# Forty-two instead of thirty-two tokens leave the dense expert grid of a PEER layer, and their expert rows are gathered in three zero-filled parts of 768 columns

## The chip, the cores and the metric

The kernel runs on one core of a Trainium2 chip. The metric is device time in microseconds (us) of one execution, the median of several. A core has TensorE (PE in the rows; its weight loads are PEld), VectorE (DVE), ScalarE (ACT), GpSimd (POOL) and SyncE (SP). SP issues the plain transfers here, POOL the gathers by index. All transfers run on the core's 16 DMA engines.

## The reference

One layer of a decoder trunk over 256 tokens of width 2048, all in float32. A token mixer (sliding-window attention and an mLSTM, gated and summed) comes first, and the change leaves it alone. Then comes PEER, a product-key retrieval of single-neuron experts:

```python
x = x + peer(rms_norm(x, norm_ffn_g), w_peer_q, peer_keys, peer_u, peer_v)

def peer(xn, w_peer_q, peer_keys, peer_u, peer_v):
    qp = (xt @ w_peer_q).reshape(T, 8, 2, 128)
    scores = einsum('thcd,hcnd->thcn', qp, peer_keys)      # 2 x 128 keys a head
    s_top, i_top = top_k(scores, 16)
    top_s, pos = top_k(sums of the two halves, 16)          # 16 of 256 pairs
    idx = ...                                               # i0 * 128 + i1, of 16384 experts
    gates = softmax(top_s)
    act = gelu(einsum('td,thkd->thk', xb, peer_u[idx]))
    return einsum('thk,thkd->td', gates * act, peer_v[idx])
```

Each token thus uses 8 x 16 = 128 of the 16384 rows of `peer_u` and of `peer_v`, each row 2048 wide.

## The kernel before

The kernel takes two ways through PEER. For most tokens it doesn't gather: it multiplies *all* 16384 rows of `peer_u` with all these tokens (the dense grid), multiplies the result with a grid of gates that is zero where a token did not choose an expert, and multiplies this grid with all of `peer_v`. The first `SP` = 32 tokens leave the grid (`ND = T - SP` = 224 stay): their 128 rows each are gathered by an indirect DMA.

**The dense grid.** `run` walks a list of units. A unit is one weight tile of 128 x 1024 floats (512 KB): SP loads it into `raw` (4 buffers, L94), ACT rounds it to `hi` (L89), DVE forms `lo = raw - hi` (L90; 2 buffers of each), and PE multiplies 8 pieces of `hi` with the tokens' high and low halves side by side (2 x ND = 448 columns) and 8 pieces of `lo` with the high half (ND = 224 columns). There are 512 units: 256 of `u` (L824, L829), then 256 of `v` (L1101, L1103). `run` emits the load and split of unit n+1 ahead of PE's work of unit n.

**What runs between.** After each unit `step` emits other work, counted by two paces: `rows_todo` (one gathered row of each of the leaving tokens; it takes `ROW` off the other pace) and `side` (choosing the experts, then `scatter`, which builds the grid of gates four tokens at a time with 4 matmuls of 128 x 128, 8 instructions on PE, L1040). In the first 92 units of `u` the choice of experts runs beside; in the other 164 `scatter` and the rows of `u`. Every fourth unit of `v` splits four rows of the grid into `ring` (`split_w`, 4 x ND elements a partition).

**The leaving tokens.** Their rows lie in `PARTS` = 4 parts of `HD` = 512 columns on 4 x 32 = 128 partitions. `fetch` gathers, for choice s, one row part a partition into one of 5 slabs; `dot` (DVE, L957) multiplies it with `own["x"]` and sums along the row; `own_weights` adds the parts with a small matmul and forms the weights; `add_row` (DVE, L983) adds the rows of `v`. There are 128 gathers of `u` and 128 of `v`; in the `v` units one every 1.81 units (`NS / (len(units) - 24)` = 128/232 a unit).

**The ends.** 40 units into the second half of `v`, `load_x1` brings back the residual in three pieces on SP's queue: tokens SP..127 (`n0` = 96 rows of 8 KB), tokens 128..255, and the leaving tokens' parts. Three units before the end `own_out` adds and stores the leaving tokens. `finish` then transposes, adds and stores the dense tokens: for each of 4 column blocks one store of `n0` rows and one of 128 rows, 2 KB a row. A plain transfer of SP waits for the eighth one before it as well (a semaphore of eight in turn).

Of the kernel before, what the change touches and what calls it, by code (L numbers as in the profile page):

```python
# [8 lines left out]
F32 = mybir.dt.float32  # L9
# [4 lines left out]
OP = mybir.AluOpType  # L14
AX = mybir.AxisListType
# [10 lines left out]
PH, NK, TOPK = 8, 128, 16  # L26
NE = NK
# [2 lines left out]
LOW = -3.0e38  # L30
HU = 1024
QU = 512
SP = 32
ND = T - SP
PARTS = P // SP
HD = D // PARTS
ROW = 0.75


@with_exitstack  # L40
def hybrid_block_kernel(ctx: ExitStack, tc: tile.TileContext, a, out):
    nc = tc.nc
    V, S, G, PE = nc.vector, nc.scalar, nc.gpsimd, nc.tensor
# [12 lines left out]
    ident = cst.tile([P, P], F32, name="ident")  # L56
# [72 lines left out]
    def step(parts, consume, rate):  # L129
# [343 lines left out]
    for t in range(NT):  # L473
        ts = slice(t * P, (t + 1) * P)
        for g in range(4):
            src = aqk[:, t, g * 256:(g + 1) * 256].rearrange("p (h d) -> p h d", d=DH)
            V.tensor_mul(src, src, rq[:, t, g * 4:(g + 1) * 4].unsqueeze(2).to_broadcast([P, 4, DH]))
            ps = psd.tile([P, QU], F32, name="sd")
# [8 lines left out]
        ps = psd.tile([P, QU], F32, name="sd")  # L487
# [237 lines left out]
    i0T = exc.tile([P, T], F32, name="i0T")  # L725
    i1T = exc.tile([P, T], F32, name="i1T")
    part = exc.tile([P, 1], F32, name="part")
    for c in range(PARTS):
        V.memset(part[c * SP:(c + 1) * SP], float(c))
    pair = exc.tile([P, SP], F32, name="pair")  # L730
    V.tensor_reduce(pair, ident.rearrange("p (c t) -> p t c", c=PARTS), axis=AX.X, op=OP.add)
    NSL = 5
    slab = [exc.tile([P, HD], F32, name=f"slab{j}") for j in range(NSL)]
    NA = 80
# [51 lines left out]
    W = [wA, None]  # L786
# [4 lines left out]
    done = {"tok": 0, "e": 0}  # L791
# [15 lines left out]
    own = {}  # L807
# [99 lines left out]

    tables = {"u": a["ur"], "v": a["v"].rearrange("e (c d) -> (e c) d", d=HD)}  # L910
# [13 lines left out]

    def fetch(table, s):
        ix = own["ix"]
        G.indirect_dma_start(out=slab[s % NSL], out_offset=None, in_=tables[table],  # L927
                             in_offset=bass.IndirectOffsetOnAxis(ap=ix[:, s:s + 1], axis=0))

    def quarter_rows(dst, src):  # L930

        for c in range(PARTS):
            G.dma_start(dst[c * SP:(c + 1) * SP], src[:, c * HD:(c + 1) * HD])

    def own_x():
        quarter_rows(own["x"], x1d[0:SP])
        g = a["grow"]
        quarter_rows(slab[NSL - 1], bass.AP(tensor=g.tensor, offset=g.offset, ap=[[0, SP], [1, D]]))

    def own_index():  # L940
        V.tensor_mul(own["x"], own["x"], slab[NSL - 1])
        ef = tk.tile([SP, NS], F32, name="ef")
        V.scalar_tensor_tensor(ef, iv[0:SP, 0], float(NK), iv[0:SP, 1], op0=OP.mult, op1=OP.add)
        G.dma_start(exd, ef)
        for c in range(PARTS):
            G.dma_start(own["ixf"][c * SP:(c + 1) * SP], exd)

    def own_rows():
        V.tensor_scalar(own["ixf"], own["ixf"], float(PARTS), part, op0=OP.mult, op1=OP.add)
        V.tensor_copy(own["ix"], own["ixf"])  # L950
        for s in range(NSL):
            fetch("u", s)
        rows_todo.extend([lambda s=s: dot(s) for s in range(NS)])

    def dot(s):
        sl = slab[s % NSL]
        (V.scalar_tensor_tensor(sl, sl, 1.0, own["x"], op0=OP.mult, op1=OP.mult,  # L957
                                    accum_out=own["dots"][:, s:s + 1]))
        if s + NSL < NS:
            fetch("u", s + NSL)  # L960

    def own_weights():
        zt, wt, wgt = own["zt"], slab[0][:, 0:NS], own["dots"]
        zp = psd.tile([P, QU], F32, name="sd")
        PE.matmul(zp[:, 0:SP], own["dots"], pair, start=True, stop=True)
        yield
        V.tensor_mul(zt, zp[:, 0:SP], rb[:, 0:SP])
        S.activation(zt, zt, AF.Gelu)
        V.tensor_mul(wt.rearrange("p (c t) -> p c t", c=PARTS), zt.unsqueeze(1).to_broadcast([P, PARTS, SP]),
                     gT[:, 0:SP].unsqueeze(1).to_broadcast([P, PARTS, SP]))  # L970
        yield
        wp = psd.tile([P, QU], F32, name="sd")
        PE.transpose(wp[:, 0:NS], wt, ident)
        V.tensor_copy(wgt, wp[:, 0:NS])
        for s in range(NSL):
            fetch("v", s)

    def add_row(s):
        w = own["dots"][:, s:s + 1]
        if s == 0:  # L980
            (V.tensor_scalar(own["x"], slab[0], w, None, op0=OP.mult))
        else:
            (V.scalar_tensor_tensor(own["x"], slab[s % NSL], w, own["x"], op0=OP.mult, op1=OP.add))  # L983
# [40 lines left out]
    TG = 4  # L1024

    def scatter(t0):

        A = eb.tile([P, TG, NK], F32, name="A")
        B = eb.tile([P, TG, NK], F32, name="B")
        V.tensor_tensor(A, iot.unsqueeze(1).to_broadcast([P, TG, NK]),  # L1030
                        i0T[:, t0:t0 + TG].unsqueeze(2).to_broadcast([P, TG, NK]), op=OP.is_equal)
        for j in range(TG):
            t = t0 + j
            S.activation(B[:, j], iot, AF.Square, bias=i1T[:, t:t + 1])
            S.activation(B[:, j], B[:, j], AF.Relu, bias=gT[:, t:t + 1], scale=ngT[:, t:t + 1])  # L1035
            if j % 2:
                yield
        ps = psd.tile([P, TG, NK], F32, name="sd")
        for j in range(TG):
            PE.matmul(ps[:, j], B[:, j], A[:, j], start=True, stop=True)  # L1040
        yield
        m = done["e"]
        c0 = t0 - SP
        for mul, s in ((False, 0), (False, 1), (True, 0), (True, 1)):
            lo, hi = ((0, NA), (NA, NE))[s]
            for x0, x1 in (((lo, min(max(m, lo), hi)),) if mul else ((max(min(m, hi), lo), hi),)):
                if x1 <= x0:
                    continue
                dst = W[s][:, x0 - lo:x1 - lo, c0:c0 + TG]
                src = ps[:, :, x0:x1].rearrange("p t i -> p i t")  # L1050
# [169 lines left out]
```

## Time and profile before

| | |
|---|---|
| median of 3 runs | 2179.22 us (2178.59 to 2179.59) |
| the profiled execution, its own time | 2179.96 us |
| its span, first to last instruction | 2178.2 us |
| PE busy, weight loads busy | 97%, 89% of the span |
| DVE, ACT, POOL busy | 77%, 60%, 18% |
| bytes moved | 487.22 MB, 224 GB/s over the span |

The span is what the rows of the trace cover; the profiled execution's own time is 1.8 us longer. Matmuls are pipelined, so PE's busy share is no measure of how far it is from its peak: its pace is read from where one matmul starts and where the next does. An engine that is busy all the time sets the pace only where others wait for it.

### The profile page before, as it was taken

The page shows a single profiled execution, that of the slowest core. Times are in us where ns is not written, and L with a number is a line of the kernel's source. Part 1 is how long each engine was busy: PE and PEld are TensorE (multiplying, and loading weights), DVE is VectorE, ACT ScalarE, POOL GpSimd, SP SyncE. Part 2 cuts the span into 40 slices and gives each one's busy share as a digit, 9 for nine tenths or more (in the row PEclk, how much of TensorE's full clock was granted, in tenths as well). Part 3 has the DMA queues.
Part 4 walks back from the last instruction along what each step waited for, and adds up shares of the span by engine and source line. Part 5 has one row for each costly group of instructions (what it writes and reads, how often), then busy time and mean ns, then how long its engine had stood idle before and what let it go on. Part 6 is the DMA issues. An engine that isn't in the chain of part 4 may idle for free. (4 is left out here: it accounts for less than half of the span.)

```text
span 2178.2 us, 34889 instructions
## 1 busy us (share of the span) xinstructions
PE 2120.5 (97%) x12836; PEld 1934.2 (89%) x12836; DVE 1685.0 (77%) x2915; ACT 1307.7 (60%) x2269; POOL 382.4 (18%) x324
## 2 busy tenths in 40 slices
PE   6999999999999999998999999999999999999997
PEld 5887778888888888997999999998999999989997
DVE  7987688878887889898777777886777777767765
ACT  5755566556644455555889888886455455545453
POOL 3000000000022002102332333321222222222200
PEclk9999999999999999999999999999999999999999
DMA  5565544555577545765777677776887777888764
GB/s 202 187 190 175 163 155 165 175 190 187 185 253 265 178 174 198 243 222 182 251 251 261 239 251 254 259 238 210 270 267 266 268 270 257 270 272 272 265 229 141
DMA packets 138892, 487.22 MB, mean 224 GB/s; under 512 B 17713, under 2 KB 19969, under 8 KB 138241
## 3 DMA queue, kind: packets, MB, share of 16 engines
q1 hardware_dynamic: 115520, 415.43, 56.0%
q0 software_dynamic: 20896, 67.73, 10.0%
q8 instruction: 100, 1.64, 0.3%
q10 hardware_dynamic: 2304, 1.84, 0.3%
q14 instruction: 72, 0.58, 0.1%
HBM read 478.88 MB, written 6.05 MB: 223 GB/s over the span
## 5 line engine op out<-in xcount | busy, mean ns | idle before, releaser
L90 DVE TENSOR_TENSOR lo<-raw,hi 128x1024 fp32r<-128x1024 f32 x762 | 936.6, 1230 | 423.2 <-ACT hi L89 416.3
L89 ACT ACTIVATE hi<-raw 128x1024 fp32r<-128x1024 f32 x762 | 804.6, 1058 | 759.5 <-PE mm L1101 312.8
L824 PE MATMUL mm<-X,hi 128*128 128x448 f32 x2048 | 467.5, 371 | 11.4 <-ACT hi L89 8.9
L824 PEld LDWEIGHTS mm<-X,hi 128*128 128x128 f32 x2048 | 367.7, 190 | 38.8 <-ACT hi L89 12.5
L1101 PE MATMUL sd<-X,hi 128*128 128x448 f32 x1024 | 378.6, 370 | 11.4 <-ACT hi L89 8.8
L1101 PE MATMUL mm<-X,hi 128*128 128x448 f32 x1024 | 376.8, 368 | 0.0
L174 PE MATMUL mm<-X,hi 128*128 128x512 f32 x1040 | 271.1, 402 | 15.1 <-ACT hi L89 8.4
L829 PEld LDWEIGHTS mm<-X,lo 128*128 128x128 f32 x2048 | 268.2, 192 | 14.2 <-DVE lo L90 7.6
L829 PE MATMUL mm<-X,lo 128*128 128x224 f32 x2048 | 270.0, 274 | 4.1 <-DVE lo L90 4.0
L1103 PE MATMUL mm<-X,lo 128*128 128x224 f32 x1024 | 243.2, 276 | 0.0
L1103 PE MATMUL sd<-X,lo 128*128 128x224 f32 x1024 | 241.3, 273 | 0.0
L174 PEld LDWEIGHTS mm<-X,hi 128*128 128x128 f32 x1040 | 189.5, 191 | 53.2 <-DVE X L90 9.0
L927 POOL DMA_INDIRECT slab<-v,oix x128 | 149.4, 1167 | 474.2 <-DVE ox L983 415.1
L927 POOL DMA_INDIRECT slab<-ur,oix x128 | 150.8, 1178 | 402.9 <-DVE slab L957 367.5
L1101 PEld LDWEIGHTS sd<-X,hi 128*128 128x128 f32 x1024 | 194.6, 190 | 23.3 <-ACT hi L89 9.2
L1101 PEld LDWEIGHTS mm<-X,hi 128*128 128x128 f32 x1024 | 194.7, 190 | 13.3
L1103 PEld LDWEIGHTS sd<-X,lo 128*128 128x128 f32 x1024 | 197.0, 192 | 3.9
L1103 PEld LDWEIGHTS mm<-X,lo 128*128 128x128 f32 x1024 | 197.0, 192 | 2.8
L178 PEld LDWEIGHTS mm<-X,lo 128*128 128x128 f32 x1040 | 142.7, 191 | 10.4
L178 PE MATMUL mm<-X,lo 128*128 128x256 f32 x1040 | 146.4, 283 | 0.0
L1035 ACT ACTIVATE B<-B,gT,ngT 128x128 f32<-128x128 f32 x224 | 110.8, 494 | 7.5
L700 POOL COPY sqa<-sq 128x256 f32<-128x256 f32 x1 | 0.9, 875 | 564.3 <-ACT sq L698 564.3
(326 smaller groups left out, 2441.4 us busy)
## 6 DMA issues: line engine op xcount, KB each, us to landing
raw<-u SPq DMA_DIRECT2D x256, 512.0 KB, 4.4
raw<-v SPq DMA_DIRECT2D x256, 512.0 KB, 4.6
raw<-w_g SPq DMA_DIRECT2D x64, 512.0 KB, 3.5
raw<-w_tok SPq DMA_DIRECT2D x56, 512.0 KB, 3.6
raw<-w_qk SPq DMA_DIRECT2D x32, 512.0 KB, 3.6
raw<-w_o SPq DMA_DIRECT2D x32, 512.0 KB, 3.8
raw<-w_pq SPq DMA_DIRECT2D x32, 512.0 KB, 3.7
raw<-w_pa SPq DMA_DIRECT2D x16, 512.0 KB, 3.2
```

The lines of the kernel that those rows point to most:

```text
L89: S.activation(hi, src, AF.Copy)
L90: V.tensor_sub(lo, src, hi.bitcast(F32))
L174: PE.matmul(ps, hi[:, w], X[:, k].rearrange("p s t -> p (s t)"), start=(k == 0), stop=False)
L178: PE.matmul(ps[:, :T], lo[:, w], X[:, k, 0], start=False, stop=(k == kts - 1))
L700: G.tensor_copy(sqa, sq)
L824: PE.matmul(ps[:, :2 * ND], hi[:, w], Xn[:, k].rearrange("p s t -> p (s t)"), start=(k == 0), stop=False)
L829: PE.matmul(ps[:, :ND], lo[:, w], Xn[:, k, 0], start=False, stop=(k == KT - 1))
L927: G.indirect_dma_start(out=slab[s % NSL], out_offset=None, in_=tables[table], in_offset=bass.IndirectOffsetOnAxis(ap=ix[:, s:s + 1], axis=0))
L1035: S.activation(B[:, j], B[:, j], AF.Relu, bias=gT[:, t:t + 1], scale=ngT[:, t:t + 1])
L1101: PE.matmul(acc[h][j][:, :2 * ND], hi[:, j * P:(j + 1) * P], both, start=(i == 0), stop=False)
L1103: PE.matmul(acc[h][j][:, :ND], lo[:, j * P:(j + 1) * P], ring[:, i % NR, 0], start=False, stop=(i == NE - 1))
```

## The change

`SP` goes from 32 to 42, so `ND` from 224 to 214. `PARTS` goes from 4 to 3 and `HD` from 512 to 768; 3 x 42 = 126 partitions (`PU`) are used. 3 x 768 = 2304 is more than 2048, so the host lays out both tables with rows filled up with zeros (`ur`, `vr`); the third part of a row holds 512 columns of data and 256 zeros, and the gather moves them all. `ROW`, the row's share in the pace, goes from 0.75 to 1.03. `part` (which part a partition holds) now comes from an iota and two comparisons, and `own["x"]` and one slab are set to zero before they are filled. `scatter` takes 214 tokens in 53 groups of four and one of two. `n0` goes from 96 to 86.

```diff
-SP = 32
+SP = 42
 ND = T - SP
-PARTS = P // SP
-HD = D // PARTS
-ROW = 0.75
+PARTS = 3
+PU = PARTS * SP
+HD = 768
+ROW = 1.03
...
-    tables = {"u": a["ur"], "v": a["v"].rearrange("e (c d) -> (e c) d", d=HD)}
+    tables = {"u": a["ur"], "v": a["vr"]}
+    ends = [(c * HD, min(c * HD + HD, D)) for c in range(PARTS)]
...
-        G.indirect_dma_start(out=slab[s % NSL], out_offset=None, in_=tables[table],
-                             in_offset=bass.IndirectOffsetOnAxis(ap=ix[:, s:s + 1], axis=0))
+        G.indirect_dma_start(out=slab[s % NSL][0:PU], out_offset=None, in_=tables[table],
+                             in_offset=bass.IndirectOffsetOnAxis(ap=ix[0:PU, s:s + 1], axis=0))
...
     def own_x():
+        V.memset(own["x"], 0.0)
+        V.memset(slab[NSL - 1], 0.0)
...
-        sl = slab[s % NSL]
-        (V.scalar_tensor_tensor(sl, sl, 1.0, own["x"], op0=OP.mult, op1=OP.mult,
-                                    accum_out=own["dots"][:, s:s + 1]))
+        sl = slab[s % NSL][0:PU]
+        V.scalar_tensor_tensor(sl, sl, 1.0, own["x"][0:PU], op0=OP.mult, op1=OP.mult,
+                               accum_out=own["dots"][0:PU, s:s + 1])
...
-            (V.scalar_tensor_tensor(own["x"], slab[s % NSL], w, own["x"], op0=OP.mult, op1=OP.add))
+            V.scalar_tensor_tensor(ox, sl, w, ox, op0=OP.mult, op1=OP.add)
...
         for c in range(PARTS):
-            nc.sync.dma_start(x1s[c * SP:(c + 1) * SP], x1d[0:SP, c * HD:(c + 1) * HD])
+            c0, c1 = ends[c]
+            nc.sync.dma_start(x1s[c * SP:(c + 1) * SP, 0:c1 - c0], x1d[0:SP, c0:c1])
...
-        "ur": z["peer_u"].reshape(PARTS * NE * P, HD),
+        "ur": fill(z["peer_u"]),
+        "vr": fill(z["peer_v"]),
```

The line numbers move with the change: L824 becomes L828, L957 L965, L983 L991, L1080 L1091, L1101 L1113, L1103 L1115, L1120 L1132.

On SP the transfers around `load_x1` stood so before (`raw` is the weight buffer, `wA` the tile whose front part the residual reuses, `x1d` the residual in DRAM):

```order
L94 DMA raw<-v 128x1024 x170
L1080 DMA wA<-x1d 96x2048
L1081 DMA wA<-x1d 128x2048
L1083 DMA wA<-x1d 32x512 x4
L94 DMA raw<-v 128x1024 x85
L1125 DMA out<-ox 32x512 x4
L94 DMA raw<-v 128x1024
L1120 DMA out<-wA 96x512
L1120 DMA out<-wA 128x512
```

and so they stand now:

```order
L95 DMA raw<-v 128x1024 x170
L1091 DMA wA<-x1d 86x2048
L1092 DMA wA<-x1d 128x2048
L1095 DMA wA<-x1d 42x768 x2
L1095 DMA wA<-x1d 42x512
L95 DMA raw<-v 128x1024 x85
L1138 DMA out<-ox 42x768 x2
L1138 DMA out<-ox 42x512
L95 DMA raw<-v 128x1024
L1132 DMA out<-wA 86x512
L1132 DMA out<-wA 128x512
```

Nothing moved in place: the same 170 and 85 loads of `v` stand around the residual. The row counts did: 96 became 86, and four pieces of 32 rows became three of 42.

On DVE a piece of the `v` units stood so before (`lo` is the split of a weight tile, `X` the split of four grid rows, `ox` the sum of the leaving tokens):

```order
L983 SCALAR_TENSOR_TENSOR ox<-slab_6803,odots,ox 128x512
L90 TENSOR_TENSOR lo<-raw,hi 128x1024
L90 TENSOR_TENSOR X<-wB,X 128x4x224
L90 TENSOR_TENSOR lo<-raw,hi 128x1024
L983 SCALAR_TENSOR_TENSOR ox<-slab_6799,odots,ox 128x512
```

and now:

```order
L991 SCALAR_TENSOR_TENSOR ox<-slab_6804,odots,ox 126x768
L91 TENSOR_TENSOR lo<-raw,hi 128x1024
L91 TENSOR_TENSOR X<-wB,X 128x4x214
L91 TENSOR_TENSOR lo<-raw,hi 128x1024
L991 SCALAR_TENSOR_TENSOR ox<-slab_6800,odots,ox 126x768
```

The order is the same; the row operation has 768 instead of 512 elements a partition, the grid split 856 instead of 896.

## Rows read from the trace of the kernel before

**Rows 1.** Page: busy; a queue's packets, MB, share; chain; issues, us to landing.

```profile
PE 2120.5 (97%) x12836; PEld 1934.2 (89%) x12836; DVE 1685.0 (77%) x2915; ACT 1307.7 (60%) x2269; POOL 382.4 (18%) x324
...
q1 hardware_dynamic: 115520, 415.43, 56.0%
...
PE sd L1101 10%; PE mm L1101 9%; PE mm L1103 5%; PE sd L1103 5%; DMA raw<-v 1%; DVE wA L1119 0%; ACT hi L89 0%; DVE wA L215 0%; SPq L1125 0%; DVE lo L90 0%; DVE ox L1123 0%; DVEq L1216 0%; DVE ox L983 0%; DVE oT L215 0%; ACT wA L214 0%
...
raw<-v SPq DMA_DIRECT2D x256, 512.0 KB, 4.6
```

**Rows 2.** Windows, three stages: busy us (instructions), clock, DMA share, GB/s.

```profile
790.00:1015.00 225.00, 220.63 (x1391) 207.31 (x1390) 206.92 (x485) 121.61 (x180) 43.19 (x24) 1.00 0.63 214
1050.00:1450.00 400.00, 394.37 (x2597) 375.26 (x2596) 316.09 (x618) 341.84 (x799) 129.34 (x110) 1.00 0.76 255
1550.00:1900.00 350.00, 349.91 (x2224) 332.84 (x2223) 256.41 (x258) 178.62 (x183) 90.13 (x77) 1.00 0.79 267
```

**Rows 3.** Timeline of PE, one unit of v: start, duration, instruction.

```profile
1700.54 0.38 PE L1101 MATMUL sd<-X,hi 128*128 128x448 f32 x1
...
1702.17 0.27 PE L1103 MATMUL sd<-X,lo 128*128 128x224 f32 x1
...
1703.05 0.38 PE L1101 MATMUL sd<-X,hi 128*128 128x448 f32 x1
```

**Rows 4.** Timeline of PE, a unit of the output projection.

```profile
621.50 2.03 PE L174 MATMUL mm<-mx__4427,hi 128*128 128x512 f32 x8
623.37 1.09 PE L178 MATMUL mm<-mx__4427,lo 128*128 128x256 f32 x8
624.30 0.38 PE L681 MATMUL sd<-ident,xt 128*128 128x128 f32 x2
```

**Rows 5.** Timeline of PE, a unit of u and a scatter.

```profile
1301.75 1.05 PE L829 MATMUL mm<-X,lo 128*128 128x224 f32 x8
1302.63 1.06 PE L1040 MATMUL sd<-A,B 128*128 128x128 f32 x8
1303.45 1.87 PE L824 MATMUL mm<-X,hi 128*128 128x448 f32 x8
```

**Rows 6.** Groups by form, 1050 to 1450: busy us, mean ns, idle before.

```profile
L824 PE MATMUL mm<-X,hi 128*128 128x448 f32 x1104 | 252.0, 370 | 5.2 <-ACT hi L89 4.7
...
L90 DVE TENSOR_TENSOR lo<-raw,hi 128x1024 fp32r<-128x1024 f32 x139 | 170.3, 1225 | 78.8 <-ACT hi L89 78.3
...
L957 DVE SCALAR_TENSOR_TENSOR slab<-slab,ox 128x512 f32<-128x512 f32 x110 | 75.1, 683 | 0.0
```

**Rows 7.** Groups by form, 1490 to 2150.

```profile
L983 DVE SCALAR_TENSOR_TENSOR ox<-slab,odots,ox 128x512 f32<-128x512 f32 x127 | 94.8, 746 | 0.0
```

**Rows 8.** Waits of PE, 780 to 1040: total us, times, longest.

```profile
PE mm L829 <- DVE lo L90: 4.0, 7, 1.5
```

**Rows 9.** Timeline of SP around the residual's load.

```profile
1924.76 0.47 SPq L1080 DMA_DIRECT2D wA<-x1d  x1
1925.27 0.49 SPq L1081 DMA_DIRECT2D wA<-x1d  x1
```

**Rows 10.** The chain that ended last, at this place.

```profile
1928.46 12.82 DMA raw<-v
1941.38 1.07 ACT hi L89
```

**Rows 11.** Windows behind it.

```profile
1938.00:1940.00 2.00, 0.00 (x0) 0.00 (x0) 0.00 (x0) 0.00 (x0) 0.00 (x0) 1.00 1.00 321
1940.00:1942.00 2.00, 0.00 (x0) 0.00 (x0) 0.00 (x0) 0.62 (x1) 0.00 (x0) 1.00 1.03 412
...
1944.00:1946.00 2.00, 2.00 (x8) 1.83 (x7) 2.00 (x3) 0.56 (x2) 0.37 (x1) 0.50 0.70 254
```

**Rows 12.** DMA, 1924 to 1942: packets; issues with KB and us to landing.

```profile
DMA packets 1436, 5.59 MB, mean 310 GB/s; under 512 B 232, under 2 KB 232, under 8 KB 1212
```

**Rows 13.** DMA, 2168 to 2179, the last stores.

```profile
DMA packets 1024, 1.84 MB, mean 167 GB/s; under 512 B 128, under 2 KB 128, under 8 KB 1024
...
out<-wA SPq DMA_DIRECT2D x4, 256.0 KB, 3.4
out<-wA SPq DMA_DIRECT2D x4, 192.0 KB, 3.1
```

**Rows 14.** Timeline of SP at the end.

```profile
2169.28 4.76 SPq L1120 DMA_DIRECT2D out<-wA  x8
```

More of the change, by code (lines that the diff above doesn't have):

```diff
@@ L727, in hybrid_block_kernel @@
     part = exc.tile([P, 1], F32, name="part")
-    for c in range(PARTS):
-        V.memset(part[c * SP:(c + 1) * SP], float(c))
+    pcol = exc.tile([P, 1], F32, name="pcol")
+    G.iota(pcol, pattern=[[0, 1]], base=0, channel_multiplier=1, allow_small_or_imprecise_dtypes=True)
+    V.tensor_scalar(part, pcol, float(SP), None, op0=OP.is_ge)
+    V.tensor_scalar(pcol, pcol, float(2 * SP), None, op0=OP.is_ge)
+    V.tensor_add(part, part, pcol)
     pair = exc.tile([P, SP], F32, name="pair")
-    V.tensor_reduce(pair, ident.rearrange("p (c t) -> p t c", c=PARTS), axis=AX.X, op=OP.add)
+    V.tensor_reduce(pair, ident[:, 0:PU].rearrange("p (c t) -> p t c", c=PARTS), axis=AX.X, op=OP.add)
     NSL = 5
@@ L926, in fetch @@
         ix = own["ix"]
-        G.indirect_dma_start(out=slab[s % NSL], out_offset=None, in_=tables[table],
-                             in_offset=bass.IndirectOffsetOnAxis(ap=ix[:, s:s + 1], axis=0))
+        G.indirect_dma_start(out=slab[s % NSL][0:PU], out_offset=None, in_=tables[table],
+                             in_offset=bass.IndirectOffsetOnAxis(ap=ix[0:PU, s:s + 1], axis=0))
     def quarter_rows(dst, src):
         for c in range(PARTS):
-            G.dma_start(dst[c * SP:(c + 1) * SP], src[:, c * HD:(c + 1) * HD])
+            G.dma_start(dst[c * SP:(c + 1) * SP, 0:ends[c][1] - ends[c][0]], src[:, ends[c][0]:ends[c][1]])
     def own_x():
+        V.memset(own["x"], 0.0)
+        V.memset(slab[NSL - 1], 0.0)
         quarter_rows(own["x"], x1d[0:SP])
@@ L940, in own_index @@
     def own_index():
-        V.tensor_mul(own["x"], own["x"], slab[NSL - 1])
+        V.tensor_mul(own["x"][0:PU], own["x"][0:PU], slab[NSL - 1][0:PU])
         ef = tk.tile([SP, NS], F32, name="ef")
@@ L948, in own_rows @@
     def own_rows():
-        V.tensor_scalar(own["ixf"], own["ixf"], float(PARTS), part, op0=OP.mult, op1=OP.add)
-        V.tensor_copy(own["ix"], own["ixf"])
+        V.tensor_scalar(own["ixf"][0:PU], own["ixf"][0:PU], float(PARTS), part[0:PU], op0=OP.mult, op1=OP.add)
+        V.tensor_copy(own["ix"][0:PU], own["ixf"][0:PU])
         for s in range(NSL):
@@ L964, in own_weights @@
         zp = psd.tile([P, QU], F32, name="sd")
-        PE.matmul(zp[:, 0:SP], own["dots"], pair, start=True, stop=True)
+        PE.matmul(zp[:, 0:SP], own["dots"][0:PU], pair[0:PU], start=True, stop=True)
         yield
@@ L968, in own_weights @@
         S.activation(zt, zt, AF.Gelu)
-        V.tensor_mul(wt.rearrange("p (c t) -> p c t", c=PARTS), zt.unsqueeze(1).to_broadcast([P, PARTS, SP]),
+        V.tensor_mul(wt[:, 0:PU].rearrange("p (c t) -> p c t", c=PARTS), zt.unsqueeze(1).to_broadcast([P, PARTS, SP]),
                      gT[:, 0:SP].unsqueeze(1).to_broadcast([P, PARTS, SP]))
@@ L972, in own_weights @@
         wp = psd.tile([P, QU], F32, name="sd")
-        PE.transpose(wp[:, 0:NS], wt, ident)
-        V.tensor_copy(wgt, wp[:, 0:NS])
+        PE.transpose(wp[0:PU, 0:NS], wt[:, 0:PU], ident)
+        V.tensor_copy(wgt[0:PU], wp[0:PU, 0:NS])
         for s in range(NSL):
@@ L978, in add_row @@
     def add_row(s):
-        w = own["dots"][:, s:s + 1]
+        w, sl, ox = own["dots"][0:PU, s:s + 1], slab[s % NSL][0:PU], own["x"][0:PU]
         if s == 0:
-            (V.tensor_scalar(own["x"], slab[0], w, None, op0=OP.mult))
+            V.tensor_scalar(ox, sl, w, None, op0=OP.mult)
         else:
-            (V.scalar_tensor_tensor(own["x"], slab[s % NSL], w, own["x"], op0=OP.mult, op1=OP.add))
+            V.scalar_tensor_tensor(ox, sl, w, ox, op0=OP.mult, op1=OP.add)
         if s + NSL < NS:
@@ L1026, in scatter @@
     def scatter(t0):
+        tg = min(TG, T - t0)
         A = eb.tile([P, TG, NK], F32, name="A")
         B = eb.tile([P, TG, NK], F32, name="B")
-        V.tensor_tensor(A, iot.unsqueeze(1).to_broadcast([P, TG, NK]),
-                        i0T[:, t0:t0 + TG].unsqueeze(2).to_broadcast([P, TG, NK]), op=OP.is_equal)
-        for j in range(TG):
+        V.tensor_tensor(A[:, 0:tg], iot.unsqueeze(1).to_broadcast([P, tg, NK]),
+                        i0T[:, t0:t0 + tg].unsqueeze(2).to_broadcast([P, tg, NK]), op=OP.is_equal)
+        for j in range(TG + 1):
+            if j in (2, TG):
+                yield
+            if j >= tg:
+                continue
             t = t0 + j
@@ L1035, in scatter @@
             S.activation(B[:, j], B[:, j], AF.Relu, bias=gT[:, t:t + 1], scale=ngT[:, t:t + 1])
-            if j % 2:
-                yield
         ps = psd.tile([P, TG, NK], F32, name="sd")
-        for j in range(TG):
+        for j in range(tg):
             PE.matmul(ps[:, j], B[:, j], A[:, j], start=True, stop=True)
@@ L1048, in scatter @@
                     continue
-                dst = W[s][:, x0 - lo:x1 - lo, c0:c0 + TG]
-                src = ps[:, :, x0:x1].rearrange("p t i -> p i t")
+                dst = W[s][:, x0 - lo:x1 - lo, c0:c0 + tg]
+                src = ps[:, 0:tg, x0:x1].rearrange("p t i -> p i t")
                 if mul:
@@ L1054, in scatter @@
                     S.activation(dst, src, AF.Copy)
-        done["tok"] = c0 + TG
+        done["tok"] = c0 + tg
     side += [(0.55, scatter(t0)) for t0 in range(SP, T, TG)]
@@ L1122, in own_out @@
     def own_out():
-        V.tensor_add(own["x"], own["x"], x1s)
+        V.tensor_add(own["x"][0:PU], own["x"][0:PU], x1s[0:PU])
         for c in range(PARTS):
-            nc.sync.dma_start(out[0:SP, c * HD:(c + 1) * HD], own["x"][c * SP:(c + 1) * SP])
+            c0, c1 = ends[c]
+            nc.sync.dma_start(out[0:SP, c0:c1], own["x"][c * SP:(c + 1) * SP, 0:c1 - c0])
     units = [(a["v"][i * P:(i + 1) * P, h * HU:(h + 1) * HU], v_consume(i, h)) for h in range(2) for i in range(NE)]
@@ L1177, in col, with fill @@
         return v.reshape(-1, P).T
+    def fill(m):
+        return np.pad(m, ((0, 0), (0, PARTS * HD - D))).reshape(-1, HD)
     wt = np.concatenate([cols(w, 0, 3), cols(w, 5, 7)], axis=1)
```

## The prediction

> **What bounds the kernel now.** I read the page first. The chain that ended last is almost wholly PE in the lines of the `v` units [rows 1], so what counts is how fast PE gets from one unit to the next, and which waits break that. The table by stage comes next [rows 2]. A unit has 16 matmuls, so 1550 to 1900 holds 2224/16 = 139 units, 2.52 us each, with no idle PE. From 1050 to 1450 there are 1104/8 = 138 units of `u` [rows 6], 2.90 us each, scatter's matmuls included, and 5.6 us of idle PE. From 790 to 1015, where the experts are chosen, DVE is busy 206.9 of 225 us, a unit takes 2.59 us, and in and around this stretch PE waited seven times for DVE's `lo` [rows 8]: there DVE is nearly as tight as PE. The transfer engines are busy 0.79 of the time at 267 GB/s in `v` [rows 2].
>
> Then PE's timeline, start to start, since a matmul's own duration is no pace. In `v`, eight matmuls of 448 columns take 1702.17 - 1700.54 = 1.63 us (204 ns each) and eight of 224 take 0.88 us (110 ns) [rows 3]. Before the grid, eight of 512 take 1.87 us (234 ns) and eight of 256 take 0.93 us (116 ns) [rows 4]. Eight of 128 columns in scatter still take 0.82 us (102 ns), beside eight of 224 in 0.88 [rows 5]. So long matmuls follow their columns, short ones hardly.
>
> **What PE saves.** Two parts to each unit:
>
> - `hi`, 448 to 428 columns. Between 448 and 512 a column costs (234 - 204)/64 = 0.47 ns, so 20 columns 9.4 ns; in proportion it is 204 x 20/448 = 9.1. I take 9.2.
> - `lo`, 224 to 214. In proportion it would be 4.9 ns; between 224 and 256 ten columns cost 2.0 ns, between 128 and 224 only (110 - 102)/96 x 10 = 0.8 ns. 214 lies in the last interval: 0.8.
>
> [...]
>
> By stage: 256 units of `v` save 20.5 us, the 164 later units of `u` 13.1. The first 92 would save 7.4; there DVE is 92% busy and gets longer rows, so I keep half, 3.7. Scatter has 53.5 groups instead of 56, 2.5 x 0.82 us = 2.0 [rows 5]. Together -39.3.
>
> **What DVE pays.** The row operation takes 683 ns for 512 elements, the split 1225 for 1024 [rows 6]: 1.06 ns an element, so 256 more cost 0.27 us; `add_row`, 746 ns now [rows 7], becomes about 1.02 us. In `v` DVE has 256.4/139 = 1.84 us a unit, plus 0.552 x 0.27 = 0.15: 1.99 of 2.43, so it hides behind PE with 0.4 us to spare. In the later `u` it has 316.1/138 = 2.29, plus 110/138 x 0.27 = 0.21: 2.50 of some 2.80, 90%. That still fits on average, but scatter's work comes in lumps and DVE works in order: an `lo` stands behind a longer row operation. I charge 4 us (0 to 10). The two memsets, the iota and comparisons: 1 us, in the stretch where DVE is tight.
>
> **What the gathers pay.** A gather grows from 262 KB to 126 x 3 KB = 387 KB; 256 of them are 32 MB more. In `v` a unit then needs 524 + 0.552 x 387 = 738 KB in 2.43 us, 304 GB/s. At 0.79 busy for 267 GB/s the engines would be full at 338, so 304 is 0.90 of them. The only stretch in which everything waits for transfers ran at 310 GB/s [rows 12], which leaves 2%. Five slabs give a gather five turns of 1.81 units, 22 us, so a later landing there stalls nobody; what is at risk is the weight tile, which lands in 4.6 us [rows 1]. It has four buffers and is issued three units ahead, 7 us: slack enough on average. I charge 2 us (0 to 10).
>
> **The row counts 86.** This is the unknown. Each large plain transfer of the `v` stage before has a row count that is a multiple of 16: 128, 96, 32 rows. The last stores show what one costs in packets: 4 x 96 + 4 x 128 = 896 rows and 1024 packets, so 128 small ones, 16 to each of eight stores [rows 13]: every one of them ended on 16 engines. 86 = 2 x 43 can't be shared evenly among 16; among engines that get the same number of whole rows it goes over two. No row shows whether the split must be even. Lower bound: as now, nothing. Upper bound: two engines.
>
> - *The residual's load.* Now its 96 rows put 6 x 8 KB on each engine. Over two engines it is 43 x 8 KB = 352 KB on each. An engine moves 412/16 = 25.7 GB/s at the best [rows 11] and 415.43 MB/(0.56 x 16 x 2178.2 us) = 21.3 on average [rows 1]: 13.7 to 16.5 us instead of about 2. The next weight tiles are queued behind it on SP's queue [rows 9]. [...] I take 10.
> - *The stores.* From SP's first issue at 2169.28 [rows 14] the span lasts 8.9 us. Over two engines the four stores of 86 rows put 4 x 43 x 2 KB = 352 KB on each, 13.7 to 16.5 us, and the four of 128 rows 64 KB more, 2.5 to 3 us. With 3.5 us for start and landing (a store lands in 3.1 us with almost nothing to move [rows 13]) that is 20 to 23 us instead of 8.9: 11 to 14. I take 12; nothing on PE can cover it, it is the end.
>
> I take the even split, since all that the rows show is even. [...]
>
> The pieces of 42 rows are small (three loads, three stores instead of four) and spare SP an issue of about 0.4 us; I count nothing.
>
> **The sum.** -39.3 + 4 + 1 + 2 + 10 + 12 = -10.3 us. The profiled execution took 2179.96 us, so 2169.7; the median of the runs is 0.7 below it: 2169. By its own bounds 2160 to 2180.
>
> **Rivals.**
>
> - *86 rows cost what 96 do.* For it: nothing in the rows shows an uneven count. Against: the same. Then the 22 us are not paid: 2147.
> - *Transfers become the bound (slower).* The `v` units need 304 GB/s, 310 were seen. Two things could lower what is to be had: rows of 3 KB over 126 partitions, and gathers that load some engines more than others. Under 304 each unit takes 738 KB/rate; slower than before it gets when `v` adds some 15 us, at 2.49 us a unit, 296 GB/s. At 290 GB/s: 2.545 us in `v`, +29, and in the later `u`, (524 + 0.80 x 387) KB/290 = 2.88 for 2.80, +13: 2211. Against it: 0.79 busy at 267.
> - *DVE becomes the bound in `u`.* At 90% with work in lumps the later `u` gains nothing (+13) and neither does the choosing stage (+4): 2186. For it: [rows 8], and PE's 5.6 us of idleness in 400 already. Against: that idleness is small and was mostly for ACT.
>
> **How the numbers follow.** 0.2% is 4.4 us, about what a measurement can tell from no change: faster is under 2174.8, slower over 2183.6. The forecast has 0.55 (0.40 faster, 0.11 same, 0.04 slower), the cheap 86 rows 0.24 (all faster), transfers as bound 0.12 (slower), DVE as bound 0.09 (0.04 same, 0.05 slower). That is 0.64, 0.15, 0.21. The range takes in the cheap rows with a little better `lo`, 2143, and DVE as bound with some longer stores, 2192; outside is most of the transfer rival.
>
> **What would show it.** Right: a `v` unit of 2.43 us start to start, `hi` matmuls 195 ns apart and `lo` 109; `add_row` at 1.02 us; the 86-row stores landing ever later, the last after 15 us or more; the wait for the weight tile behind the residual 20 us or more. Wrong: `lo` at 105 (saves 8 us more); 86-row stores that land in 3 us (22 us faster); ACT waiting for `raw` again and again in `v`, with 300 GB/s or less (transfers); PE waiting for `lo` through the whole of `u` (DVE).

## The result and the profile after

The changed kernel takes 2265.19 us (median of four executions, 2256.30 to 2273.73), the kernel before 2179.40 us (2178.59 to 2182.02) on the same chip: the ratio is 1.0391, 95% interval 1.0369 to 1.0413. It is 3.9% slower, where 0.5% faster was forecast. The profiled execution took 2273.73 us, its span is 2272.0.

The page of the kernel after, its lines of busy time, queues, chain and issues (compare [rows 1]):

```profile
PE 2120.4 (93%) x12816; PEld 1946.9 (86%) x12816; DVE 1743.3 (77%) x2911; ACT 1296.0 (57%) x2244; POOL 420.4 (19%) x322
...
DMA packets 142819, 519.22 MB, mean 229 GB/s; under 512 B 20142, under 2 KB 22374, under 8 KB 142178
...
q1 hardware_dynamic: 115352, 415.34, 59.5%
q0 software_dynamic: 24992, 99.90, 17.4%
...
DMA 21%; PE 19%; ACT 8%; DVE 5%; issue 1%; POOL 0%; ACTq 0%; SPq 0%; DVEq 0%
...
raw<-u SPq DMA_DIRECT2D x256, 512.0 KB, 6.6
raw<-v SPq DMA_DIRECT2D x256, 512.0 KB, 7.6
```

PE's busy total is the same as before, but its share fell, and the chain that ended last, which was almost wholly PE, now has more of the transfer engines than of PE. A weight tile of `v` lands in 7.6 us instead of 4.6. The windows of the three stages say where (busy us of PE, weight loads, DVE, ACT, POOL, then clock, DMA share, GB/s; before: [rows 2]):

```profile
790.00:1015.00 225.00, 215.85 (x1378) 206.65 (x1376) 205.82 (x485) 119.58 (x180) 43.08 (x28) 0.99 0.68 221
1050.00:1450.00 400.00, 362.93 (x2347) 346.62 (x2346) 307.92 (x553) 304.45 (x707) 122.60 (x100) 0.99 1.00 262
1550.00:1900.00 350.00, 337.05 (x2139) 323.91 (x2138) 262.56 (x250) 171.43 (x177) 103.69 (x72) 1.00 1.00 281
```

From 1050 on the transfer engines are busy all the time, at 262 and 281 GB/s; before they carried 267 GB/s at a share of 0.79. A `v` unit takes 350/(2139/16) = 2.62 us, where the pace of PE alone would be 2.45. ACT's waits from 1040 to the end (total us, times, longest) name what is late:

```profile
ACT hi L90 <- DMA raw<-v: 241.0, 130, 23.7
...
ACT hi L90 <- DMA raw<-u: 62.8, 40, 3.7
```

Every second tile of `v` is waited for (130 of 256). By stage, from the first matmul of one unit to that of another (us, worked out from PE's timeline; the last column is `e3_both`, a kernel that comes below, with both of the change's odd row counts taken out):

| stage | before | after | `e3_both` |
|---|---|---|---|
| first 92 units of `u` | 244.5 | 247.8 | 246.9 |
| later 164 units of `u` | 482.6 | 518.3 | 469.3 |
| first 128 units of `v` | 323.6 | 335.7 | 315.5 |
| last 128 units of `v` | 330.8 | 362.6 | 327.5 |
| from there to the end | 16.2 | 27.3 | about 16 |

The five differences from before to after add up to 94 us, the difference of the two spans. Two pieces of them are not the general lack of transfers. One is the residual, whose 86 rows were issued at 1981.99; a tile behind them made ACT wait 23.75 us, where 8.24 were waited at this place before (timeline of ACT, in the kernel before and then in the kernel after; in brackets the idle time ahead and its cause):

```profile
1941.38 1.06 ACT L89 ACTIVATE hi<-raw 128x1024 fp32r<-128x1024 f32 x1 [8.24 <-DMA raw<-v]
```

```profile
2013.91 1.06 ACT L90 ACTIVATE hi<-raw 128x1024 fp32r<-128x1024 f32 x1 [23.75 <-DMA raw<-v]
```

The other is the end. SP issues the first store at 2251.82, and the span goes on for 20.2 us, 11.3 more than before [rows 14]. Windows of the last microseconds:

```profile
2264.00:2268.00 4.00, 0.00 (x0) 0.00 (x0) 0.00 (x0) 0.00 (x0) 0.00 (x0) 0.50 0.14 53
2268.00:2270.00 2.00, 0.00 (x0) 0.00 (x0) 0.00 (x0) 0.00 (x0) 0.00 (x0) 0.50 0.13 51
```

A share of 0.13 of 16 engines is two engines, and 52 GB/s are 26 for each: the stores of 86 rows do go over two engines.

### The profile page after: what moved, and what is told of

Read it like the earlier page. It is cut to its first block, busy times and chain, and to the rows that moved or that the text cites. A ratio compares the mean times of both kernels' runs of the same rounds, so it can differ in the third digit from the quotient of the medians.

```text
span 2272.0 us, 34813 instructions
## 1 busy us (share of the span) xinstructions
PE 2120.4 (93%) x12816; PEld 1946.9 (86%) x12816; DVE 1743.3 (77%) x2911; ACT 1296.0 (57%) x2244; POOL 420.4 (19%) x322
## 3 DMA queue, kind: packets, MB, share of 16 engines
q10 hardware_dynamic: 2304, 1.75, 0.2%
## 4 chain that ended last, share of the span: by engine, by line
DMA 21%; PE 19%; ACT 8%; DVE 5%; issue 1%; POOL 0%; ACTq 0%; SPq 0%; DVEq 0%
DMA raw<-v 14%; DMA raw<-u 8%; ACT hi L90 5%; PE sd L1113 4%; PE mm L828 4%; PE mm L1113 4%; DVE lo L91 3%; PE mm L833 2%; PE mm L1115 2%; PE sd L1115 2%; ACT B L1048 1%; ACT B L1047 1%; PE sd L1051 1%; DVE ox L991 0%; POOL oh L888 0%
## 5 line engine op out<-in xcount | busy, mean ns | idle before, releaser
L828 PE MATMUL mm<-X,hi 128*128 128x428 f32 x2048 | 456.5, 365 | 40.6 <-ACT hi L90 38.3
L1113 PE MATMUL sd<-X,hi 128*128 128x428 f32 x1024 | 379.3, 370 | 52.5 <-ACT hi L90 48.1
L828 PEld LDWEIGHTS mm<-X,hi 128*128 128x128 f32 x2048 | 368.3, 190 | 61.7 <-ACT hi L90 47.0
L1113 PE MATMUL mm<-X,hi 128*128 128x428 f32 x1024 | 370.2, 362 | 0.0
L833 PEld LDWEIGHTS mm<-X,lo 128*128 128x128 f32 x2048 | 270.5, 193 | 17.3 <-DVE lo L91 13.9
L833 PE MATMUL mm<-X,lo 128*128 128x214 f32 x2048 | 271.9, 276 | 9.2 <-DVE lo L91 9.0
L933 POOL DMA_INDIRECT slab<-vr,oix x128 | 179.2, 1400 | 488.5 <-DVE ox L991 433.7
L1113 PEld LDWEIGHTS sd<-X,hi 128*128 128x128 f32 x1024 | 196.3, 192 | 68.3 <-ACT hi L90 56.5
L1115 PE MATMUL mm<-X,lo 128*128 128x214 f32 x1024 | 244.6, 276 | 0.0
L1115 PE MATMUL sd<-X,lo 128*128 128x214 f32 x1024 | 241.8, 274 | 0.0
L933 POOL DMA_INDIRECT slab<-ur,oix x128 | 159.1, 1243 | 433.8 <-DVE slab L965 420.3
L1113 PEld LDWEIGHTS mm<-X,hi 128*128 128x128 f32 x1024 | 196.0, 191 | 5.9
L1115 PEld LDWEIGHTS sd<-X,lo 128*128 128x128 f32 x1024 | 197.9, 193 | 2.4 <-DVE lo L91 0.4
L1115 PEld LDWEIGHTS mm<-X,lo 128*128 128x128 f32 x1024 | 198.0, 193 | 1.9
L991 DVE SCALAR_TENSOR_TENSOR ox<-slab,odots,ox 126x768 f32<-126x768 f32 x127 | 128.4, 1011 | 0.0
L965 DVE SCALAR_TENSOR_TENSOR slab<-slab,ox 126x768 f32<-126x768 f32 x128 | 123.6, 965 | 0.0
```

Of the source, the lines that this page charges most:

```text
L828: PE.matmul(ps[:, :2 * ND], hi[:, w], Xn[:, k].rearrange("p s t -> p (s t)"), start=(k == 0), stop=False)
L833: PE.matmul(ps[:, :ND], lo[:, w], Xn[:, k, 0], start=False, stop=(k == KT - 1))
L933: G.indirect_dma_start(out=slab[s % NSL][0:PU], out_offset=None, in_=tables[table], in_offset=bass.IndirectOffsetOnAxis(ap=ix[0:PU, s:s + ...
L965: V.scalar_tensor_tensor(sl, sl, 1.0, own["x"][0:PU], op0=OP.mult, op1=OP.mult, accum_out=own["dots"][0:PU, s:s + 1])
L991: V.scalar_tensor_tensor(ox, sl, w, ox, op0=OP.mult, op1=OP.add)
L1113: PE.matmul(acc[h][j][:, :2 * ND], hi[:, j * P:(j + 1) * P], both, start=(i == 0), stop=False)
```

## The experiments

The times are medians, and each ratio, with its 95% interval in brackets, is to runs of the kernel before on the same chip (medians 2178.8 to 2180.7 us). The expectations name theories by a letter. A is that the number of engines counts: it assumes that 126 rows reach 14 of the 16 engines, and that these fill first. C, formed later, is that the number of rows itself counts: a transfer of other than 128 rows and the 128-row transfers beside it cost each other time, also on 16 engines. It supposes that the shares of such a transfer lie otherwise on the engines and partitions, which no trace here shows. Their rival, B, is that the bytes alone filled the engines; for `e4_before126` B says that nothing changes.

**The two odd counts, one at a time and together.** In `e1_gather128` the gathers fetch 128 rows instead of 126. The two spare partitions fetch a row of the table that nothing reads. (Of the diffs in this section only the part that matters is shown; here one more slab is zeroed and the row numbers are formed on all 128 partitions.)

```diff
-        G.indirect_dma_start(out=slab[s % NSL][0:PU], out_offset=None, in_=tables[table],
-                             in_offset=bass.IndirectOffsetOnAxis(ap=ix[0:PU, s:s + 1], axis=0))
+        G.indirect_dma_start(out=slab[s % NSL], out_offset=None, in_=tables[table],
+                             in_offset=bass.IndirectOffsetOnAxis(ap=ix[:, s:s + 1], axis=0))
```

> The changed kernel, with each gather over 128 instead of 126 partitions (the two spare ones fetch a valid row part that nothing reads): 1.6% more bytes, and a row count that is a multiple of 16. Theory A (spread): the gathers of 126 rows run on 14 engines instead of 16 and these 14 fill up; with 128 the waits of ACT for raw (241 us for raw<-v, 63 us for raw<-u) go almost wholly, but for the one behind the residual, and the time falls by 50 to 65 us from 2265, to 2200 to 2215. Theory B (bytes): the 32 MB more are too much however they are spread; 2255 to 2275.

Measured: 2176.29 us, ratio 0.9986 (0.9976 to 0.9996). Two more rows in a gather, 1.6% more bytes in it, take 89 us off the changed kernel and bring it level with the one before. That is B refuted, and more than the 50 to 65 us that A gave.

In `e2_split86` the gathers stay at 126 rows; the residual's 86 rows and each store of 86 rows go as 80 and 6.

```diff
-        nc.sync.dma_start(x1[0:n0, 0], x1d[SP:P])
+        nc.sync.dma_start(x1[0:80, 0], x1d[SP:SP + 80])
+        nc.sync.dma_start(x1[80:n0, 0], x1d[SP + 80:P])
...
+            for r0, r1 in ((0, 80), (80, n0)) if t == 0 else ((0, P),):
+                nc.sync.dma_start(out[(P if t else SP) + r0:(P if t else SP) + r1, cols], o[r0:r1])
```

> The changed kernel, with each transfer of 86 rows cut into one of 80 and one of 6 rows (the residual's load and the four stores); the gathers stay at 126 partitions. If 86 rows go over two engines, as the last stores of the changed kernel look, the 23 us wait behind the residual falls to about 8 and the end shortens by 10 us: some 25 us in all, 2235 to 2245. If the long wait behind the residual is owed to the gathers' load and not to the 86 rows, only the end shortens: 2252 to 2258.

Measured: 2244.51 us, 1.0284 (1.0267 to 1.0301). That is 20.7 us less than the changed kernel; ACT still waits 131 times for `raw` of `v`; the longest wait, the one behind the residual, is 13.3 us, where some 8 were expected.

`e3_both` has both edits.

> Both edits, gathers over 128 partitions and 86 rows as 80 + 6. Theory A (spread): what is left is the change as predicted without the 86 rows, 2145 to 2165, faster than before. Theory B (bytes): 2230 to 2245, as with the 86 rows cut alone.

Measured: 2155.48 us, 0.9880 (0.9863 to 0.9896). The two edits add up: 20.8 us from `e1_gather128` to here, 89.0 from `e2_split86`. Windows of `e3_both`, the same two stages:

```profile
1050.00:1450.00 400.00, 392.47 (x2619) 380.82 (x2618) 343.42 (x619) 339.15 (x793) 139.22 (x112) 1.00 0.84 294
1550.00:1900.00 350.00, 349.92 (x2271) 340.28 (x2270) 281.06 (x265) 180.96 (x185) 90.45 (x78) 1.00 0.90 302
```

and ACT's wait for the tiles of `v`, 1040 to the end:

```profile
ACT hi L90 <- DMA raw<-v: 21.0, 5, 10.0
```

More bytes a second than in the changed kernel, 302 for 281, and the engines still have a tenth of their time free. So the bytes are not what filled them. The queues of 1550 to 1900 make a price of this (packets, MB, share of 16 engines). In the kernel after:

```profile
q1 hardware_dynamic: 19105, 69.57, 68.0%
q0 software_dynamic: 7056, 28.42, 31.2%
```

and in `e3_both`:

```profile
q1 hardware_dynamic: 20421, 74.38, 61.2%
q0 software_dynamic: 6277, 30.83, 28.1%
```

A share of 16 engines over 350 us is 5600 engine-us. Queue q1 carries the weight tiles; they cost 0.680 x 5600/69.57 = 54.7 engine-us a MB beside 126-row gathers and 46.1 beside 128-row gathers, though nothing of them changed. The gathers on q0 cost 61.5 and 51.0. Both got about a fifth dearer.

**126 rows in the kernel before.** `e4_before126` gathers 126 of the 128 rows there.

> The kernel before (32 tokens, 512 columns), with each gather over 126 of its 128 partitions; it leaves out the fourth part of the last two of these tokens' rows. Fewer bytes, and a row count that 14 divides and 16 does not. Theory A: the landing of a gather gets longer (5.0 us before) and the DMA share rises from 0.79; at the lower load of this kernel some of it still hides: 2180 to 2210. Theory B: no change, 2178 to 2182, with the gathers landing as before.

Measured: 2183.71 us, 1.0016 (1.0006 to 1.0027). In `v` the DMA share goes from 0.79 to 0.86 at the same rate (266 GB/s). Windows of `e4_before126` (before: [rows 2]):

```profile
1550.00:1900.00 350.00, 349.91 (x2225) 332.85 (x2224) 256.35 (x259) 178.84 (x182) 92.39 (x76) 1.00 0.86 266
```

A gather of `v` lands in 5.8 us instead of 5.0. So part of the price is there without the change, and the slack of the transfer engines hides it almost wholly: worked out as above, a weight tile costs 50.9 engine-us a MB for 46.4 in the kernel before, about half of the rise in the kernel after.

**Fewer rows: engines or rows?** Two kernels take `e2_split86` and gather fewer of the rows: 120 (15 engines with 8 each, by A) and 112 (16 engines with 7 each); the sums run over the same rows.

```diff
-        G.indirect_dma_start(out=slab[s % NSL][0:PU], out_offset=None, in_=tables[table],
-                             in_offset=bass.IndirectOffsetOnAxis(ap=ix[0:PU, s:s + 1], axis=0))
+        G.indirect_dma_start(out=slab[s % NSL][0:112], out_offset=None, in_=tables[table],
+                             in_offset=bass.IndirectOffsetOnAxis(ap=ix[0:112, s:s + 1], axis=0))
```

> The changed kernel with 86 rows as 80 + 6, and each gather over the first 120 of the 126 partitions; it leaves out the third part of the last six of the leaving tokens. 120 rows share evenly over 15 engines, 8 rows each as with 128. If it is the even sharing over fewer than 16 engines that costs, it stays well over the 2155 of the kernel with both edits though it moves 6% less: 2185 to 2235. If it is the nine rows an engine, or the raggedness of 126, it is as fast: 2148 to 2160.

Measured: 2243.23 us, 1.0311 (1.0276 to 1.0346): no better than 126 rows, with 5% fewer bytes in the gathers, and 8 us above the range of the first case.

> The same with the first 112 of the 126 partitions; it leaves out the third part of the last fourteen of the leaving tokens. 112 rows share evenly over 16 engines, 7 rows each. If the number of engines decides: as fast as with 128, 2145 to 2157. If a gather has to cover all 128 partitions to be fast: over 2200.

Measured: 2179.05 us, 0.9996 (0.9982 to 1.0011). A is missed by over 20 us: by A sixteen engines with equal shares, an eighth fewer bytes gathered than in `e3_both`, and it is 24 us slower. The other case, over 2200, is missed by as much: 112 rows cost less time than 120 or 126. The sizes of the gather queue's packets in `v` fit the shares that A assumed: a gather of 126 rows has 56 packets of two rows and 14 of one (fourteen engines with nine rows each), one of 120 has 60 of two (fifteen with eight), one of 112 has 48 of two and 16 of one (sixteen with seven). So the packets fit even shares, and still the price stayed: a weight tile of `v` costs 54.6 engine-us a MB, as above (0.709 x 5600/72.69). Windows of `e6_gather112`:

```profile
1550.00:1900.00 350.00, 346.94 (x2239) 336.11 (x2237) 275.50 (x260) 177.77 (x182) 108.22 (x77) 1.00 1.01 284
```

The engines are full at 284 GB/s. From here on C was the theory. `e11_gather64` gathers the first 64 rows (16 engines with four each, by A), half of the bytes.

> The changed kernel with 86 rows as 80 + 6, and each gather over the first 64 of the 126 partitions (it leaves out half of the row parts): 16 engines, 4 rows each, half the bytes. Theory C: at some 250 GB/s in v a DMA share that is higher than the same rate has in the kernels with 128 partitions (0.89 at 302 GB/s, 339 GB/s at a share of one): over 0.80. Theory A: 0.74 or less. The time says little, since half the bytes fit in either case: 2145 to 2165.

Measured: 2158.19 us, 0.9907 (0.9886 to 0.9928). Windows of `e11_gather64`:

```profile
1550.00:1900.00 350.00, 349.92 (x2269) 340.25 (x2268) 280.13 (x264) 181.49 (x186) 91.00 (x78) 1.00 0.90 258
```

The same share as with 128 rows (0.90), for 258 instead of 302 GB/s. The bytes that fell away paid for what the others got dearer; PE is not held up, so the time tells little and the share tells it.

**The weight tiles themselves.** If C holds, it must show in the kernel before with its gathers as they are, when the weight tiles get another row count. `e10_raw112` loads each tile as 112 and 16 rows.

```diff
-        nc.sync.dma_start(raw, src)
+        nc.sync.dma_start(raw[0:112], src[0:112])
+        nc.sync.dma_start(raw[112:P], src[112:P])
```

> The kernel before, with every weight tile loaded as 112 and 16 rows instead of 128 at once; the gathers stay as they were (128 partitions). The bytes and the packet sizes are the same, all 16 engines work, but 7 rows an engine fall on other partitions than 8. Theory C (which engine writes which partitions decides): the DMA share rises at the same rate in stages without any gather too, from 0.54 between 450 and 500 us to 0.62 or more, and the v units at 267 GB/s get waits for raw; 2190 to 2260. Theory A (only the number of engines counts, 16 here): 2178 to 2188, share as before.

Measured: 2293.53 us, 1.0522 (1.0504 to 1.0541). That is more than C's range. The share rose without gathers too, but less than expected: from 0.54 to 0.59 between 450 and 500, from 0.46 to 0.52 between 300 and 400. And the edit has a second effect, twice the issues and landings. Two further kernels of the same shape separate the two: the tile as two transfers of 512 columns on all 128 rows, and as two transfers of 64 rows.

```diff
-        nc.sync.dma_start(raw, src)
+        nc.sync.dma_start(raw[:, 0:512], src[:, 0:512])
+        nc.sync.dma_start(raw[:, 512:1024], src[:, 512:1024])
```

> The kernel before, with each weight tile loaded as two transfers of 128 rows by 512 columns instead of one of 128 by 1024: as many issues and landings as with 112 + 16 rows, but every transfer has 128 rows. If the rows per transfer are what takes capacity (theory C), 2170 to 2200 us with an unstalled v at 0.80 to 0.86 DMA share, since 2 KB pieces may cost the engines a little. If twice the issues, landings and semaphore waits were what cost 5.2% with 112 + 16 rows, about 2290 us again and several hundred us of waits for raw.

Measured: 2180.51 us, 1.0004 (0.9993 to 1.0015). Twice the issues and pieces of half the length cost no time; in `v` a tile takes 47.6 engine-us a MB for 46.4.

```diff
-        nc.sync.dma_start(raw, src)
+        nc.sync.dma_start(raw[0:64], src[0:64])
+        nc.sync.dma_start(raw[64:P], src[64:P])
```

> The kernel before, with each weight tile loaded as two transfers of 64 rows by 1024 columns: 16 engines with four rows each, 4 KB a piece as before, twice the issues. Theory C (a row count other than 128 beside 128-row gathers): the v stage gets a share of 0.95 or more at 240 to 280 GB/s and the time goes over 2220 us. If only an uneven number of rows (16 rows in a transfer, 14 engines) costs, or issues cost nothing: 2175 to 2195 us at 0.79 to 0.82.

Measured: 2331.27 us, 1.0710 (1.0677 to 1.0743). The queue of the weight tiles from 300 to 400, where no gathers run and PE is busy 98.9% of the time or more in all four kernels. In the kernel before:

```profile
q1 hardware_dynamic: 4430, 16.12, 46.0%
```

in `e12_cols512`:

```profile
q1 hardware_dynamic: 8923, 16.25, 46.2%
```

in `e10_raw112`:

```profile
q1 hardware_dynamic: 4875, 16.04, 51.9%
```

and in `e13_rows64`:

```profile
q1 hardware_dynamic: 4909, 16.05, 60.0%
```

The same bytes at the same pace take 46, 46, 52 and 60% of the engines: worked out as above (a share of 16 engines over 100 us is 1600 engine-us) 45.7, 45.5, 51.8 and 59.8 engine-us a MB. In `v` the engines of `e13_rows64` are full at 235 GB/s, and in `u`, from 1050 to 1450, at 228:

```profile
1050.00:1450.00 400.00, 373.60 (x2393) 349.45 (x2392) 297.15 (x549) 313.24 (x712) 119.06 (x97) 1.00 0.99 228
```

Rows in a transfer count, issues and columns (almost) don't. No gather is needed for it: two transfers of 64 rows that follow each other are enough.

**Smaller rows, shorter sums.** Both kernels build on `e3_both`. `e8_hd688` makes the parts 688 columns wide (3 x 688 = 2064 still holds 2048).

```diff
-HD = 768
+HD = 688
```

> Both edits (128 partitions, 80 + 6 rows), and parts of 688 instead of 768 columns (3 x 688 = 2064, 16 zeros instead of 256): a gather moves 352 KB instead of 393, a row operation has 80 elements less. If bytes and VectorE's rows still cost something once the gathers run on 16 engines, 3 to 8 us less than the 2155 of both edits: 2147 to 2152. If both hide, 2152 to 2158.

Measured: 2152.21 us, 0.9881 (0.9855 to 0.9906), the lowest median of all. But it is not shown to be faster than `e3_both`: the ratio is the same (0.9881 and 0.9880), and the executions overlap (2150.2 to 2153.0 and 2152.3 to 2157.5). Nor do the 3 us lie where rows are gathered: the first 92 units of `u` take 243.7 us for 246.9, the later `u` 468.3 for 469.3, the two halves of `v` together 643.8 for 643.0. Bytes and row operations hide.

`e9_dot512` sums only the first 512 of the 768 columns in `dot`, to see what DVE's longer rows cost in `u`.

```diff
-        V.scalar_tensor_tensor(sl, sl, 1.0, own["x"][0:PU], op0=OP.mult, op1=OP.mult,
+        V.scalar_tensor_tensor(sl[:, 0:512], sl[:, 0:512], 1.0, own["x"][0:PU, 0:512], op0=OP.mult, op1=OP.mult,
```

> Both edits, and dot over the first 512 of the 768 columns of a part; it leaves out the rest of each sum. VectorE's row operation on u is then as long as before the change, the bytes stay. If VectorE eats what the choosing stage and the later u should have saved, 4 to 9 us less than 2155: 2146 to 2151. If what is missing there are waits for transfers, 2152 to 2158.

Measured: 2153.14 us, 0.9884 (0.9858 to 0.9911). The later `u` takes 469.3 us, as in `e3_both`: DVE's 768 columns don't hold it up. Waits for transfers don't either: ACT has none for the tiles of `u` there, in `e3_both` as in `e9_dot512`.

## Why the prediction was wrong

**The step that failed** is "What the gathers pay", its last sentence: "I charge 2 us (0 to 10)". It cost about 89 us. The step added up the bytes rightly, 304 GB/s wanted in `v`, and divided them by 338 GB/s, a capacity that was worked out from a stage in which every transfer had 128 rows. `e3_both` shows that this was right for 128 rows: 302 GB/s at a share of 0.90, that is 336. With 126-row gathers the capacity is the 281 GB/s at which the engines are full. The prediction weighed an uneven row count, and priced it, for the 86 rows alone. Its case for the gathers rested on bytes, where the row count made the price of a byte.

**The rival "transfers become the bound"** is what happened, and its formula holds once the rate is known: 738 KB/281 GB/s = 2.63 us a unit of `v`, 2.62 were seen; in the later `u` (524 + 0.80 x 387) KB/262 GB/s = 3.18, and 518.3/164 = 3.16 were seen. (The rates are those of the same stretches, so this tests the bytes of a unit.) It had a chance of 0.12 and a point from which it decides, 296 GB/s; only the rate was unknown (2211 us was for 290 GB/s). Of its two reasons the rows of 3 KB are cleared by `e1_gather128`. That some engines get more than others is at most a part: with 112 and 64 rows (32 packets of two) the packets fit equal shares on all sixteen, and the price of a byte is as high as with 126 (54.6, 54.3 and 54.7 engine-us a MB for a weight tile).

**What makes a byte dearer** is shown as far as this: a transfer of 126, 120, 112 or 64 rows takes more engine time a byte than one of 128, and the 128-row transfers beside it do too (54 to 55 for 46 engine-us a MB in `v` with 126, 120, 112 and 64 rows of 3 KB, 51 with 126 rows of 2 KB, worked out alike from their queues); columns, pieces of 2 KB and the number of transfers hardly do (`e12_cols512`: 47.6 for 46.4 in `v`, 45.5 for 45.7 from 300 to 400). The single packets say when. In `v` of the kernel after, a weight tile's packet of 4 KB that starts while a gather's data are under way takes 241 ns on average, any other 187; in `e6_gather112` it is 244 and 185, in `e11_gather64` 250 and 200, in `e3_both`, with more bytes a second, 184 and 193. So the tiles get dearer while such a gather runs, and hardly otherwise. What was not tried is 128 rows that fall on other engines, so the number of rows and the places where its shares fall are not told apart. How the shares of a transfer meet inside the chip no trace here shows, so the reason there stays open.

**The row counts 86** were right in mechanism and size: +10 and +12 forecast, 20.8 us measured by `e1_gather128` against `e3_both` and 20.7 by the changed kernel against `e2_split86`. The rival "86 rows cost what 96 do" is out: a share of 0.13, two engines. The stores' part was 11.3 us for 12. For the residual the 10 us were the author's estimate; the wait behind it is 15.5 us longer than before (23.75 for 8.24), and the longest wait goes from 22.0 us in `e1_gather128` to 10.0 in `e3_both`.

**What PE saves** was mis-sized. PE's timeline of the kernel after, a unit that waits for nothing (compare [rows 3]):

```profile
1555.56 0.37 PE L1113 MATMUL sd<-X,hi 128*128 128x428 f32 x1
...
1557.13 0.26 PE L1115 MATMUL sd<-X,lo 128*128 128x214 f32 x1
...
1558.01 0.37 PE L1113 MATMUL sd<-X,hi 128*128 128x428 f32 x1
```

Eight `hi` take 1.57 us (196 ns each, 195 forecast), eight `lo` 0.88, as with 224 columns: nothing saved there. The 0.8 ns that the prediction took for `lo` came from scatter's 102 ns. That is the time from the first of its eight matmuls to the next group, divided by eight; inside the group one starts every 112 ns (median), the same as with 224 columns; with 214 it is 111. A unit saves 2.51 - 2.45 = 0.06 us; the medians of all units of `v`, 2.513 before and 2.460 in `e3_both`, give 0.053, not the 0.08 that 9.2 + 0.8 ns make eight times over. The range by the forecast's own bounds, 2160 to 2180, starts from a least saving a unit that no run shows; the runs showed less, the 0.053. Over 256 and 164 units that is 6.9 and 4.4 us less than forecast. The choosing stage, of which half the gain was kept, shows none: 244.5 us before, and 244.6, 246.9, 243.7 and 245.2 in `e1_gather128`, `e3_both`, `e8_hd688` and `e9_dot512`. DVE's busy time there is 206 of 225 us before and after; that DVE is the cause was not tried.

**What DVE pays.** The row operation takes 1.01 us in `add_row`, 1.02 were forecast; lines of the kernel after by group (busy us, mean ns):

```profile
L991 DVE SCALAR_TENSOR_TENSOR ox<-slab,odots,ox 126x768 f32<-126x768 f32 x127 | 128.4, 1011 | 0.0
L965 DVE SCALAR_TENSOR_TENSOR slab<-slab,ox 126x768 f32<-126x768 f32 x128 | 123.6, 965 | 0.0
```

The charge of 4 us for it was not paid: in `e3_both` the later `u` is 13.3 us shorter than before, 8.7 by 53 ns a unit and about 2 by scatter, and `e9_dot512` leaves it there. The rival "DVE becomes the bound in `u`" is out with that.

**The sum without both row counts** was -39.3 + 4 + 1 + 2 = -32.3 us; `e3_both` has -25.3 by the medians and -22.5 by the two profiled executions, which can be compared by stage: `v` -11.4 for -18.5 forecast, the later `u` -13.3 for -11.1, the choosing stage +2.4 for -2.7, the end as before. In `v` PE's smaller gain is nearly all of it. Of the 2 us for the gathers it can only be said that the three units behind the residual take 16.7 us for 13.9 before; whether the gathers' load or the cut into 80 and 6 does that was not tried. That the sum comes near is in part luck, since too much was counted for PE and for DVE.

## What to carry to other kernels

Where the transfer engines are nearly full (0.90 in `v` of `e3_both`), give a transfer that runs beside a stream of 128-row tiles 128 rows too, even if some of them fetch what nothing reads: two spare rows were worth 89 us here, against some 3 in the kernel before with its slack (`e4_before126`). And 86 rows cut into 80 and 6 were worth another 21. Look at a change of shape as a change of row counts first and of bytes second. A capacity worked out from a rate and a busy share holds only for the shapes that made it (338 GB/s here from 128-row transfers, 281 with 126-row gathers); when a change brings a new shape, put the price of a byte in doubt, not only the number of bytes.

## What the hardware showed unexpectedly

The weight tiles, which the change leaves alone, cost 19% more engine time a byte (46.1 to 54.7 engine-us a MB) because of the shape of the gathers beside them. Half of the bytes gathered on 64 rows kept the engines as busy as all of them on 128 (0.90 both, 258 and 302 GB/s). Cutting a tile along its columns was free (1.0004), cutting it along its rows cost 5.2% at 112 + 16 and 7.1% at 64 + 64. And matmuls of 214 columns came no faster than those of 224, 110 ns each, nor did scatter's of 128 columns (112 from one start to the next).
